# A two-layer diffusion backbone with expert lookup: one-hot products and low parts move from GpSimd to VectorE, one h tile in the second layer, own tokens finished in the last blocks

## The chip, the core and the metric

One core of a Trainium2 chip runs the whole program in one launch. The metric is the device time of that launch in microseconds (us). Engines are named as in the profile: PE is TensorE (PEld its weight loads), DVE is VectorE, ACT is ScalarE, POOL is GpSimd, SP is the engine that issues most DMAs. Every engine takes its instructions in order.

## The reference, cut to what matters

512 latent tokens and 256 context tokens, 1024 wide, pass two layers. Each layer has a mixer (attention and a gated delta net, not touched by the change) and then this lookup among 16384 experts; the second layer runs the lookup on the latent tokens alone.

```
q = (h @ wq).reshape(N, 8, 2, 128)
s = einsum('nhpd,hpkd->nhpk', q, keys)
top_s, top_i = top_k(s, 16)
cand_s = top_s[:, :, 0, :, None] + top_s[:, :, 1, None, :]
cand_i = top_i[:, :, 0, :, None] * 128 + top_i[:, :, 1, None, :]
best_s, best_pos = top_k(cand_s, 16)
idx, gate = take(cand_i, best_pos), softmax(best_s)
u, v = u_tab[idx], v_tab[idx]
act = gelu(einsum('tnd,td->tn', u, h))
f = einsum('tn,tnd->td', gate * act, v)
x = x + mod[5] * f
```

After the second layer the output is an RMSNorm of the latent x.

## The kernel before, in words

After the mixer, `merge` writes h (normed and modulated) transposed, as two float32r tiles, a high part and the rest: `h2hi/h2lo` for the first `nd` tiles of 128 tokens and `hghi/hglo` for the last `NG[l]` tiles (2 of 6 in the first layer, 1 of 4 in the second). Every product with h is three matmuls: high by high, low by high, high by low.

The tiles are treated in two ways. For the `nd` "dense" tiles the product of h with all 16384 expert rows is formed in 128 blocks of 128 experts (`peer_h`), and weighted by a dense gate matrix G that is mostly zero. For the last `NG[l]` "own" tiles the 128 chosen rows of each token are fetched by indirect DMA (`fetch`, issued by GpSimd), first rows of u with a row product on VectorE (`own_u`, tile `gb` or `gc`, L181), then rows of v with small matmuls (`own_v`).

The lookup of a layer (`peer`) has these stages:

- `scores`: 16 products of h with wq, each followed by products with the keys on PE and a top 16 on DVE.
- routing: for each tile `select` (DVE, with 14 small operations `rt__`, `rst` on GpSimd) picks 16 of the candidates per head; for a dense tile `spread` then builds its G: per 8 tokens four one-hot operations of 128x1024 halves (tile `oh`: two comparisons, two products), 16 small matmuls, and copies out by ACT. Every second of these groups has one product on GpSimd. `tick(2)` after each group moves the row fetches on by two.
- in the same stretch the first 80 blocks are multiplied ahead (`peer_h` with `lo_on="g"`): load 512 KB (`uraw`), `uhi` on ACT, `ulo` on GpSimd, 24 matmuls into bank `ip` or `sc`, gelu, store to DRAM (`He`).
- the main loop: 64 pairs of blocks, 24 pairs with their `peer_h`, 40 read back; each gives weights `Wh/Wl` and rows `vh/vl` and is multiplied out into PSUM (tiles 0 and 1 stay in banks `at`, `sc`; the others are added to `acc` on DVE). `due` spreads the remaining fetches over the loop.
- the end: the last two pairs are multiplied tile by tile, the result is gated and added to x and normed, in the order own tiles first, then moved and stayed tiles.

A scheduler fixes the order of the instructions on each engine when the program is built, from the order of the code and the life of the buffers; the `order` excerpts below show its results. Buffers `uhi`, `ulo` are two deep, `uraw` eight, `gb` three.

Of the kernel before, what the change touches and what calls it, by code (L numbers as in the profile page):

```python
# [108 lines left out]
class Ker:  # L109
# [234 lines left out]
    def norm_tile(self, pool, x, A, shift, hi, lo, toff, hi_on="v", lo_on="v", rows=None):  # L344

        ss = self.sm(1)
        sq = self.t(pool, [128, D], "nsq", bufs=1)
# [5 lines left out]
        y = self.t(pool, [128, D], "nxn", bufs=1)  # L353
        self.ts(y, x, r, None, ALU.mult)
# [656 lines left out]
    def merge(self, l, full, T, left, later, Gad, AT, BT, xin, xm, h2, S, N):  # L1011
# [4 lines left out]
        with ExitStack() as el:  # L1016
# [83 lines left out]
            hT = []  # L1100
            for st, nm, n in ((h2, "h2", nd), (hg, "hg", NG[l])):
                hp = st.enter_context(P(nm, S))
                hT.append([self.t(hp, [128, NCH, n * 128], f"{nm}{k}", F32R) for k in ("hi", "lo")])
            with P("mgo", S) as po:
# [22 lines left out]
                for i in range(nt):  # L1127
# [9 lines left out]
                    if i >= nd:  # L1137
                        rows[i] = self.t(self.dp, [128, D], f"hrow{l}_{i}")
                    seg, j = (hT[0], i) if i < nd else (hT[1], i - nd)
                    self.norm_tile(po, x, self.As[l][g][1], self.mods[l][g][:, 24:32], *seg, j * 128, rows=rows.get(i))  # L1140
# [3 lines left out]
    def scores(self, l, hT, T, tops, topi, N):  # L1144
# [4 lines left out]
        with ExitStack() as es:  # L1149
            qp = es.enter_context(self.tc.tile_pool(name=self.nm("rq"), bufs=1, side=N))  # L1150
            wp = es.enter_context(self.tc.tile_pool(name=self.nm("wq"), bufs=1, side=N))
            segs = ((hT[0], 0, T[0]), (hT[1], 512, T[1]))

# [94 lines left out]
    def spread(self, pool, ixs, gate, i, Gd, tick):  # L1248
# [19 lines left out]
        for half in range(2):  # L1268
            stg = self.t(pool, [128, 128, 64], "stg", bufs=2)
            for t8 in range(8):  # L1270
# [102 lines left out]
    def peer(self, l, hT, h2, hg, rows, groups, ahead, near, S, N):  # L1373
# [12 lines left out]
        with ExitStack() as es:  # L1386
# [4 lines left out]
            with P("rt", N) as pool:  # L1391
# [8 lines left out]
                with P("rt2", N) as rp:  # L1400
# [42 lines left out]
            W, Vv = [], []  # L1443
            units = ng * 256
            began = state[0]
            for n, b0 in enumerate(order):
# [10 lines left out]
                if n == len(order) - 2:  # L1457
# [5 lines left out]
                    for g, _, off in groups:  # L1463
                        for o in (0, 512):
                            gx = gates[g, o] = self.adw()
                            self.load(gx, self.gate_src(l, g, 5)[:, o:o + 512])
                            for i in moved:
                                if where[i][0] == g:
                                    a = acc[:, i - moved[0], o:o + 512]
                                    self.tt(a, a, gx, ALU.mult, eng=self.G)  # L1470
                if n < len(order) - 1:
                    W, Vv = [], []
# [42 lines left out]
            for i in range(nd):  # L1515
# [3 lines left out]
                else:  # L1519
                    x = self.t(self.wp, [128, D], "uraw", bufs=2)  # L1520
                self.load(x, xd[k * 128:(k + 1) * 128, :])
# [8 lines left out]
            fp = es.enter_context(tc.tile_pool(name=self.nm("pf"), bufs=1, side=S))  # L1530
            if last:
                fg = self.t(fp, [128, D], "fgrow")
                self.load(fg, self.I["fg"].broadcast_to([128, D]))
            todo = list(range(nd, nt)) + [i for j in range(max(len(moved), len(stay))) for i in (moved[j:j + 1] + [j] * (j < len(stay)))]
            banks = iter(("tp", "ip") * 2)
            ready = {}
            for n in range(nt + 1):
                if n < nt:
                    i = todo[n]
                    g, xd, k = where[i]  # L1540
                    x = ready[i] = self.t(fp, [128, D], "fx", bufs=3)
                    if i >= nd:
                        self.load(x, outs[i])
                        xs[i] = self.t(fp, [128, D], "fxr", bufs=2)
                        self.load(xs[i], xd[k * 128:(k + 1) * 128, :])
                        po = [(x[:, o:o + 512], o) for o in (0, 512)]
                    elif i in stay:
                        po = [(sums[i][:, o:o + 512], o) for o in (0, 512)]
                    else:
                        bank = next(banks)  # L1550
                        po = [(self.psum(bank), o) for o in (0, 512)]
                    for p, o in po:
                        if i < nd:
                            self.blocks(p, W, Vv, i, o, first=i not in stay)
                        self.tt(x[:, o:o + 512], p, gates[g, o], ALU.mult)
                        self.tt(x[:, o:o + 512], x[:, o:o + 512], xs[i][:, o:o + 512], ALU.add)
                if n == 0:
                    continue
                i = todo[n - 1]
                x = ready.pop(i)  # L1560
                g, _, k = where[i]
                if last:
                    sq = self.t(fp, [128, D], "nsq", bufs=2)
                    ss = self.sm(1)
                    self.act(sq, x, AF.Square, accum=ss)
                    self.ts(ss, ss, 1.0 / D, EPS, ALU.mult, ALU.add)
                    r = self.sm(1)
                    self.rsqrt(r, ss, 1)
                    self.stt(sq, x, r, fg, ALU.mult, ALU.mult)
                    self.load(self.out[k * 128:(k + 1) * 128, :], sq)  # L1570
                else:
                    self.load(xo[g][k * 128:(k + 1) * 128, :], x)
                    self.norm_tile(fp, x, self.As[l + 1][g][0], self.mods[l + 1][g][:, 0:8], nxt[0], nxt[1],
                                   i * 128, "s", "g" if n < nt else "v")
            main.close()
# [34 lines left out]
```

## Time and profile before

| | us |
|---|---|
| median of 3 runs (6343.70 to 6354.41) | 6346.27 |
| the profiled execution | 6341.51 |
| its span | 6339.7 |

| engine | busy us | share of the span |
|---|---|---|
| PE | 5720.0 | 90% |
| DVE | 4283.3 | 68% |
| POOL | 2542.7 | 40% |
| ACT | 2408.9 | 38% |

The profiled execution is 4.8 us under the median. A share of the whole span is a mean over stages: scores and routing of the first layer run from about 1415 to 2335 us of the span, its main loop to 3555 and its end to 3606; in the second layer scores begin at 4737, routing at 4886, the main loop at 5516, the end at 6302.

### The profile page before, as it was taken

Reading aid. Unit: us, or ns where it says so; the run is one execution under the profiler, and the core shown is the slowest. Engines: PE = TensorE matmul, PEld = TensorE weight load, DVE = VectorE, ACT = ScalarE, POOL = GpSimd, SP = SyncE. Lnnn points to the kernel's source line nnn. Section 1 sums busy time; section 2 is a strip of 40 time slices with the busy share of each in tenths; the row PEclk is TensorE's granted clock in tenths of the full one; section 3 lists DMA queues with packets and bytes.
Section 4 is the critical chain, followed back from the end, with each engine's and each line's share of the span. In section 5 each row is a group of like instructions: output and inputs, shape, how many; then the busy total and the mean of one; then the engine's idle time right before and its main releaser. Section 6 shows DMA issues by size and latency. Waiting matters only on the chain. (4 is left out here: it accounts for less than half of the span.)

```text
span 6339.7 us, 99239 instructions
## 1 busy us (share of the span) xinstructions
PE 5720.0 (90%) x36471; PEld 4739.1 (75%) x36471; DVE 4283.3 (68%) x8878; ACT 2408.9 (38%) x4336; POOL 2542.7 (40%) x2049
## 2 busy tenths in 40 slices
PE   8899999998877789999999798999998766899998
PEld 6888888786666667666666588888877766787776
DVE  5989875245889946665644589888555897555455
ACT  4554444232234522222332355444532343233333
POOL 2334333222687653333433333434432876602221
PEclk9999999999988899999999899999999888999999
DMA  5442323631466689999888444322431667867885
GB/s 193 137 144 95 99 87 115 212 115 56 155 222 245 228 301 319 326 331 315 307 295 287 161 163 137 109 95 95 137 132 62 203 223 299 291 204 270 275 274 195
DMA packets 567720, 1253.59 MB, mean 198 GB/s; under 512 B 65920, under 2 KB 228416, under 8 KB 565440
## 3 DMA queue, kind: packets, MB, share of 16 engines
q1 hardware_dynamic: 456640, 844.54, 39.6%
q0 software_dynamic: 110592, 402.70, 18.0%
q8 instruction: 287, 4.70, 0.3%
q14 instruction: 201, 1.65, 0.1%
HBM read 1049.76 MB, written 197.23 MB: 197 GB/s over the span
## 5 line engine op out<-in xcount | busy, mean ns | idle before, releaser
L167 POOL TENSOR_TENSOR wlo<-wraw,whi 128x512 fp32r<-128x512 f32 x418 | 570.7, 1369 | 1348.3 <-ACT whi L189 1205.2
L160 PE MATMUL ip<-hhi,whi 128*128 128x256 f32 x3120 | 734.3, 292 | 27.8 <-ACT ev L185 24.6
L160 PE MATMUL ip<-hlo,whi 128*128 128x256 f32 x3120 | 734.4, 291 | 0.0
L160 PE MATMUL ip<-hhi,wlo 128*128 128x256 f32 x3120 | 727.8, 291 | 5.7 <-POOL wlo L167 5.6
L160 PE MATMUL ip<-h2hi,ulo 128*128 128x512 f32 (+1 forms) x1408 | 537.1, 381 | 48.7 <-POOL ulo L167 47.9
L160 PE MATMUL ip<-h2hi,uhi 128*128 128x512 f32 (+1 forms) x1408 | 534.8, 380 | 44.6 <-ACT uhi L189 43.8
L181 DVE SCALAR_TENSOR_TENSOR gb<-gb,ghr 128x1024 f32<-128x1024 f32 x293 | 437.2, 1502 | 191.7 <-DMA gb<-in_ur_dram,gix 189.7
L160 PEld LDWEIGHTS ip<-hhi,whi 128*128 128x128 f32 x3120 | 519.4, 192 | 42.4 <-ACT ev L185 28.8
L160 PEld LDWEIGHTS ip<-hhi,wlo 128*128 128x128 f32 x3120 | 519.7, 192 | 16.6 <-POOL wlo L167 7.1
L160 PE MATMUL ip<-h2lo,uhi 128*128 128x512 f32 (+1 forms) x1408 | 528.2, 375 | 0.0
L160 PEld LDWEIGHTS ip<-hlo,whi 128*128 128x128 f32 x3120 | 522.1, 192 | 8.1 <-issue 0.2
L1294 POOL DMA_INDIRECT gc<-in_v_dram,gixT x221 | 243.6, 1102 | 656.0 <-PE tp L160 505.4
L1294 POOL DMA_INDIRECT gb<-in_ur_dram,gix x293 | 360.7, 1231 | 329.3 <-DVE gb L181 218.7
L167 DVE TENSOR_TENSOR acc<-acc,tp 128x512 f32<-128x512 f32 x366 | 247.8, 684 | 348.2 <-PE tp L160 311.9
L189 ACT CAST uhi<-uraw 128x1024 fp32r<-128x1024 f32 x256 | 268.7, 1051 | 549.2 <-PE ip L160 299.8
L167 POOL TENSOR_TENSOR ulo<-uraw,uhi 128x1024 fp32r<-128x1024 f32 x160 | 395.2, 2471 | 115.4 <-ACT uhi L189 112.7
L189 ACT CAST whi<-wraw 128x512 fp32r<-128x512 f32 x418 | 258.3, 621 | 474.7 <-PE at L160 188.1
L189 ACT CAST Wh<-ge 128x512 fp32r<-128x512 f32 (+1 forms) x256 | 144.5, 566 | 629.7 <-PE tp L160 294.9
L167 DVE TENSOR_TENSOR vl<-vraw,vh 128x1024 fp32r<-128x1024 f32 x256 | 311.7, 1232 | 76.1 <-ACT vh L189 75.4
L160 PEld LDWEIGHTS ip<-h2hi,ulo 128*128 128x128 f32 x1408 | 275.5, 196 | 113.2 <-POOL ulo L167 62.0
L160 PEld LDWEIGHTS ip<-h2hi,uhi 128*128 128x128 f32 x1408 | 276.8, 197 | 98.6 <-ACT uhi L189 49.5
L1294 POOL DMA_INDIRECT gb<-in_v_dram,gixT x163 | 179.1, 1099 | 418.0 <-PE tp L160 332.3
(455 smaller groups left out, 15469.4 us busy)
## 6 DMA issues: line engine op xcount, KB each, us to landing
uraw<-in_u_dram SPq DMA_DIRECT2D x256, 512.0 KB
vraw<-in_v_dram SPq DMA_DIRECT2D x256, 512.0 KB
wraw<-in_w_in_dram SPq DMA_DIRECT2D x288, 256.0 KB
G<-stg SPq DMA_DIRECT2D x14, 4096.0 KB
g<-G SPq DMA_DIRECT2D x896, 64.0 KB
adw<-in_w_ada_dram SPq DMA_DIRECT2D x192, 256.0 KB
raw<-ev SPq DMA_DIRECT2D x80, 384.0 KB
He<-ge SPq DMA_DIRECT2D x80, 256.0 KB
```

The lines of the kernel that those rows point to most:

```text
L160: self.PE.matmul(out, lhsT, rhs, start=start, stop=stop, skip_group_check=True, **k)
L167: (eng or self.V).tensor_tensor(out, a, b, op)
L181: eng.scalar_tensor_tensor(out, a, s, b, op0, op1, accum_out=accum)
L189: self.S.copy(hi, src)
L1294: self.G.indirect_dma_start(b, None, src, bass.IndirectOffsetOnAxis(ap=ix, axis=0))
```

## The change

- `merge`, `scores`: where all tiles fit 512 columns (the second layer), h is one pair of tiles and each wq product one 512-wide matmul instead of one of 384 and one of 128 columns.
- `spread`: all one-hot products on DVE; one or two fetches per group in turn instead of two.
- routing: `ulo` of the 80 blocks ahead on DVE instead of GpSimd.
- the end: own tiles are loaded, gated, added to x and normed (`norm_scale`) before the last two pairs; only their transposes (`norm_turn`) stay behind. In the end the dense tiles come first.

```diff
     def norm_tile(...):
+        r = self.norm_scale(x, self.t(pool, [128, D], "nsq", bufs=1))
+        y = self.t(pool, [128, D], "nxn", bufs=1)
+        self.ts(y, x, r, None, ALU.mult)
+        self.norm_turn(pool, y, A, shift, hi, lo, toff, hi_on, lo_on, rows)
...
# merge
-            for st, nm, n in ((h2, "h2", nd), (hg, "hg", NG[l])):
+            whole = nt * 128 <= 512
+            for st, nm, n in ((h2, "h2", nt),) if whole else ((h2, "h2", nd), (hg, "hg", NG[l])):
...
# scores
-            segs = ((hT[0], 0, T[0]), (hT[1], 512, T[1]))
+            segs = ((hT[0], 0, T[0]), (hT[1], 512, T[1])) if len(hT) > 1 else ((hT[0], 0, TT),)
...
# spread
-                self.tt(o4[:, 2], o4[:, 1], every(3, t), ALU.mult, eng=self.G if t8 % 2 else V)
+                self.tt(o4[:, 2], o4[:, 1], every(3, t), ALU.mult)
...
-                tick()
+                tick(1 + t8 % 2)
...
# peer
-                        self.spread(rp, *self.select(rp, tops[:, i], topi[:, i]), i, Gd, lambda: tick(2))
+                        self.spread(rp, *self.select(rp, tops[:, i], topi[:, i]), i, Gd, tick)
                 for b in range(ahead):
-                    ge = self.peer_h(l, b, hT, TT, lo_on="g")
+                    ge = self.peer_h(l, b, hT, TT)
...
# peer, ahead of the last two pairs
+                    for i in range(nd, nt):
+                        g, xd, k = where[i]
+                        x = own_y[i] = self.t(ap, [128, D], "gc", bufs=4)
+                        self.load(x, outs[i])
+                        x2 = self.t(self.gp, [128, D], "gb", bufs=3)
+                        self.load(x2, xd[k * 128:(k + 1) * 128, :])
+                        for o in (0, 512):
+                            self.tt(x[:, o:o + 512], x[:, o:o + 512], gates[g, o], ALU.mult)
+                        self.tt(x, x, x2, ALU.add)
+                        r = self.norm_scale(x, self.t(self.gp, [128, D], "gb", bufs=3))
...
+                            self.load(xo[g][k * 128:(k + 1) * 128, :], x)
+                            self.ts(x, x, r, None, ALU.mult)
...
# peer, the end
-            todo = list(range(nd, nt)) + [i for j in ...]
+            own = list(range(nd, nt))
+            todo = [i for j in range(max(len(moved), len(stay))) for i in (moved[j:j + 1] + [j] * (j < len(stay)))]
+            for n, i in enumerate(todo):
+                product(i)
+                if n:
+                    if own:
+                        turn(own.pop(0))
+                    finish(todo[n - 1])
```

GpSimd, first layer, while G is built (`ulo`, `oh` as above; `rst`, `rt__` are select's). Before:

```order
L1294 DMA gb_19865<-in_ur_dram,gix_18940 128x1024
L174 TENSOR_SCALAR rt__3779_19754<-rp_19751 128x128
L167 TENSOR_TENSOR ulo_22421<-uraw_22422,uhi_22420 128x1024
L167 TENSOR_TENSOR rst_19753<-rst_19753,rt__3779_19754 128x128
L1294 DMA gb_19893<-in_ur_dram,gix_18940 128x1024
L167 TENSOR_TENSOR oh_19230<-oh_19230,rdup_19186 128x1024
L174 TENSOR_SCALAR rt__3779_19754<-rp_19751 128x128
L1294 DMA gb_19896<-in_ur_dram,gix_18940 128x1024
L167 TENSOR_TENSOR ulo_22456<-uraw_22457,uhi_22455 128x1024
```

The changed program, same place:

```order
L1302 DMA gb_20508<-in_ur_dram,gix_18940 128x1024
L1302 DMA gb_20534<-in_ur_dram,gix_18940 128x1024
L174 TENSOR_SCALAR rt__3865_20315<-rp_20312 128x128
L1302 DMA gb_20537<-in_ur_dram,gix_18940 128x1024
L167 TENSOR_TENSOR rst_20314<-rst_20314,rt__3865_20315 128x128
```

The fetches no longer share their queue with `ulo` and `oh`; select's small operations stay.

DVE, first layer, while G is built. Before:

```order
L167 TENSOR_TENSOR oh_20050<-iota_68,rdup_19798 128x1024 x2
L179 SCALAR_TENSOR_TENSOR rk_3981_20970<-rp_20969,rk_3981_20970 128x128
L181 SCALAR_TENSOR_TENSOR gb_20442,ghc_19223<-gb_20442,ghr_19221 128x1024
L167 TENSOR_TENSOR oh_20050<-oh_20050,rdup_19798 128x1024
L179 SCALAR_TENSOR_TENSOR rk_3981_20970<-rp_20969,rk_3981_20970 128x128
L167 TENSOR_TENSOR oh_20019<-oh_20019,rdup_19798 128x1024
```

The changed program:

```order
L181 SCALAR_TENSOR_TENSOR gb_21122,ghc_19223<-gb_21122,ghr_19221 128x1024
L167 TENSOR_TENSOR ulo_23095<-uraw_23096,uhi_23094 128x1024
L167 TENSOR_TENSOR oh_19983<-oh_19983,rdup_19774 128x1024
L1218 MATCH_REPLACE rc_3952_20878<-rbs_20840,rcand_20830 128x50
L1218 MATCH_REPLACE rc_3953_20884<-rbs_20840,rcand_20830 128x50
L167 TENSOR_TENSOR oh_20014<-iota_68,rdup_19774 128x1024 x2
L167 TENSOR_TENSOR oh_19955<-oh_19955,rdup_19774 128x1024
```

`ulo` now stands among the one-hot operations and behind row products `gb`. In the first layer 76 `ulo` stand ahead of the last `oh` (25 of them ahead of the first), with 110 row products; in the second 30 stand among the top 16 of `scores`, 56 between there and the last `oh` (six of the 86 belong to the main loop), with 88 row products.

PE, second layer, in `scores` (`whi`, `wlo` are wq, `at` its bank). Before:

```order
L160 MATMUL at_49104<-hglo_47422,whi_49098 128x128
L160 MATMUL at_49104<-hghi_47421,wlo_49099 128x128
L160 MATMUL at_49156<-keys_49090,rq_49153 128x128 x4
L160 MATMUL at_49201<-h2hi_47416,whi_49189 128x384
L160 MATMUL at_49201<-h2lo_47417,whi_49189 128x384
```

The changed program:

```order
L160 MATMUL at_48579<-h2lo_47413,whi_48573 128x512
L160 MATMUL at_48579<-h2hi_47412,wlo_48574 128x512
L160 MATMUL ip_51457<-h2hi_47412,ulo_51452 128x384
L160 MATMUL ip_51457<-h2hi_47412,uhi_51451 128x384
L160 MATMUL ip_51457<-h2lo_47413,uhi_51451 128x384
```

Blocks multiplied ahead (`ip<-h2hi,ulo`) now stand between the 16 steps of `scores`; before, all 80 stood behind them. Behind the last one-hot matmul of the stage stood 16 blocks in the first layer and 32 in the second; now 5 and none.

## Rows read from the trace of the kernel before

**Rows 1.** Windows: stretch, us; busy PE, PEld, DVE, ACT, POOL; PEclk; DMA; GB/s

```profile
1620.00:2335.00 715.00, 574.10 (x2960) 455.76 (x2960) 591.35 (x1123) 272.14 (x293) 511.19 (x334) 0.89 0.69 239
1797.00:2195.00 398.00, 311.06 (x1846) 250.72 (x1844) 378.86 (x536) 177.30 (x180) 283.27 (x174) 0.87 0.65 229
2335.00:3555.00 1220.00, 1193.21 (x5396) 806.38 (x5397) 687.38 (x971) 341.35 (x485) 435.46 (x387) 0.99 0.87 304
4737.00:4886.00 149.00, 121.09 (x820) 116.20 (x817) 71.52 (x480) 34.68 (x75) 35.12 (x28) 0.99 0.18 58
4886.00:5516.00 630.00, 457.83 (x2715) 429.99 (x2716) 505.26 (x850) 228.62 (x261) 476.99 (x294) 0.86 0.71 248
5316.00:5516.00 200.00, 146.06 (x721) 137.08 (x721) 115.46 (x131) 49.30 (x65) 160.44 (x97) 0.90 0.93 329
5516.00:6302.00 786.00, 785.38 (x3921) 633.14 (x3920) 419.02 (x559) 289.80 (x413) 138.69 (x129) 1.00 0.75 250
```

**Rows 2.** DVE groups, 1620 to 2335: count | busy us, mean ns | idle before

```profile
L181 DVE SCALAR_TENSOR_TENSOR gb<-gb,ghr 128x1024 f32<-128x1024 f32 x125 | 188.2, 1516 | 80.8 <-DMA gb<-in_ur_dram,gix 80.4 <-DVE gb L181 0.4
L167 DVE TENSOR_TENSOR oh<-iota,rdup 128x1024 f16<-128x1024 f16 x128 | 135.6, 1106 | 10.9 <-ACT rdup L1258 5.8 <-PE at L160 2.7 <-PE tp L160 2.4
L167 DVE TENSOR_TENSOR oh<-oh,rdup 128x1024 f16<-128x1024 f16 x96 | 102.6, 1088 | 4.1 <-POOL oh L167 3.9
...
L179 DVE SCALAR_TENSOR_TENSOR rk<-rp,rk 128x128 f32<-128x128 f32 x42 | 27.2, 648 | 0.1
```

**Rows 3.** DVE groups, second layer, 4886 to 5516

```profile
L181 DVE SCALAR_TENSOR_TENSOR gb<-gb,ghr 128x1024 f32<-128x1024 f32 x106 | 173.4, 1649 | 91.2 <-DMA gb<-in_ur_dram,gix 91.0
L167 DVE TENSOR_TENSOR oh<-iota,rdup 128x1024 f16<-128x1024 f16 x96 | 101.2, 1101 | 4.0 <-PE at L160 2.4 <-PE tp L160 1.4
L167 DVE TENSOR_TENSOR oh<-oh,rdup 128x1024 f16<-128x1024 f16 x72 | 77.2, 1097 | 3.7 <-POOL oh L167 3.6
L181 DVE SCALAR_TENSOR_TENSOR gc<-gc,ghr 128x1024 f32<-128x1024 f32 x18 | 34.3, 1935 | 12.3 <-DMA gc<-in_ur_dram,gix 9.9 <-ACT ge L185 2.4
```

**Rows 4.** Instructions by tile, whole span: count, ns min/median/max, first and last start

```profile
L167 DVE TENSOR_TENSOR oh<-iota,rdup x224: 666/681/5119, 1797.3 to 5303.2; 128x1024 f16<-128x1024 f16 x112
...
L181 DVE SCALAR_TENSOR_TENSOR gb<-gb,ghr x293: 1197/1219/5697, 1677.7 to 5526.5; 128x1024 f32<-128x1024 f32 x147
...
L179 DVE SCALAR_TENSOR_TENSOR rk<-rp,rk x70: 265/290/3416, 1641.4 to 5134.6; 128x128 f32<-128x128 f32 x70
...
L167 DVE TENSOR_TENSOR ulo<-uraw,uhi x96: 1214/1226/1293, 2334.1 to 6252.1; 128x1024 fp32r<-128x1024 f32 x96
...
L160 PE MATMUL at<-keys,rq x320: 275/275/377, 1440.8 to 4886.8; 128*128 128x128 f32 x160
```

**Rows 5.** Timeline of DVE and POOL, 2000 to 2030: start, us, instruction

```profile
2001.19 3.74 DVE L167 TENSOR_TENSOR oh<-iota,rdup 128x1024 f16<-128x1024 f16 x2
2004.85 1.21 DVE L167 TENSOR_TENSOR re<-re,rti 128x2048 f16<-128x2048 f16 x1
...
2001.06 2.45 POOL L167 TENSOR_TENSOR ulo<-uraw,uhi 128x1024 fp32r<-128x1024 f32 x1
...
2004.53 1.23 POOL L1294 DMA_INDIRECT gb<-in_ur_dram,gix  x1
```

**Rows 6.** DVE groups in the main loop of the first layer, 2335 to 3555

```profile
L181 DVE SCALAR_TENSOR_TENSOR gc<-gc,ghr 128x1024 f32<-128x1024 f32 x73 | 88.9, 1220 | 32.3 <-DMA gc<-in_ur_dram,gix 32.3
```

**Rows 7.** PE timeline, 512-wide matmuls in an unbroken run of the main loop

```profile
3519.64 0.39 PE L160 MATMUL at<-vl,Wh 128*128 128x512 f32 x1
...
3525.08 0.39 PE L160 MATMUL tp<-vh,Wl 128*128 128x512 f32 x1
```

**Rows 8.** Chain that ended last, second layer: start, us, a 384-wide block

```profile
5616.21 4.19 PE ip L160 x24
```

**Rows 9.** DVE timeline at the two layers' ends

```profile
3563.12 1.29 DVE L167 TENSOR_TENSOR fx<-fx,adw 128x512 f32<-128x512 f32 x2 [5.47 <-DMA fx<-own]
...
6311.60 1.29 DVE L167 TENSOR_TENSOR fx<-fx,adw 128x512 f32<-128x512 f32 x2 [5.70 <-DMA fx<-own]
```

More of the change, by code (lines that the diff above doesn't have):

```diff
@@ L344, in norm_tile, with norm_scale @@
     def norm_tile(self, pool, x, A, shift, hi, lo, toff, hi_on="v", lo_on="v", rows=None):
+        r = self.norm_scale(x, self.t(pool, [128, D], "nsq", bufs=1))
+        y = self.t(pool, [128, D], "nxn", bufs=1)
+        self.ts(y, x, r, None, ALU.mult)
+        self.norm_turn(pool, y, A, shift, hi, lo, toff, hi_on, lo_on, rows)
+    def norm_scale(self, x, sq):
         ss = self.sm(1)
-        sq = self.t(pool, [128, D], "nsq", bufs=1)
         self.act(sq, x, AF.Square, accum=ss)
@@ L352, in norm_tile, with norm_turn @@
         self.rsqrt(r, v, 1)
-        y = self.t(pool, [128, D], "nxn", bufs=1)
-        self.ts(y, x, r, None, ALU.mult)
+        return r
+    def norm_turn(self, pool, y, A, shift, hi, lo, toff, hi_on="v", lo_on="v", rows=None):
         for c0 in (0, 4):
@@ L1138, in merge @@
                         rows[i] = self.t(self.dp, [128, D], f"hrow{l}_{i}")
-                    seg, j = (hT[0], i) if i < nd else (hT[1], i - nd)
+                    seg, j = (hT[0], i) if whole or i < nd else (hT[1], i - nd)
                     self.norm_tile(po, x, self.As[l][g][1], self.mods[l][g][:, 24:32], *seg, j * 128, rows=rows.get(i))
@@ L1444, in peer @@
             units = ng * 256
+            own_y, fg = {}, {}
             began = state[0]
@@ L1470, in peer @@
                                     self.tt(a, a, gx, ALU.mult, eng=self.G)
+                    if last:
+                        for o in (0, 512):
+                            fg[o] = self.adw()
+                            self.load(fg[o], self.I["fg"][:, o:o + 512].broadcast_to([128, 512]))
+                    for i in range(nd, nt):
[4 more added lines that the diff above has]
+                        self.load(x2, xd[k * 128:(k + 1) * 128, :])
+                        for o in (0, 512):
+                            self.tt(x[:, o:o + 512], x[:, o:o + 512], gates[g, o], ALU.mult)
+                        self.tt(x, x, x2, ALU.add)
+                        r = self.norm_scale(x, self.t(self.gp, [128, D], "gb", bufs=3))
+                        if last:
+                            for o in (0, 512):
+                                self.stt(x[:, o:o + 512], x[:, o:o + 512], r, fg[o], ALU.mult, ALU.mult)
+                            self.load(self.out[k * 128:(k + 1) * 128, :], x)
+                        else:
+                            self.load(xo[g][k * 128:(k + 1) * 128, :], x)
+                            self.ts(x, x, r, None, ALU.mult)
                 if n < len(order) - 1:
@@ L1519, in peer @@
                 else:
-                    x = self.t(self.wp, [128, D], "uraw", bufs=2)
+                    x = self.t(ap, [128, D], "gc", bufs=4)
                 self.load(x, xd[k * 128:(k + 1) * 128, :])
@@ L1530, in peer @@
             fp = es.enter_context(tc.tile_pool(name=self.nm("pf"), bufs=1, side=S))
[L1531 to L1560, printed above, removed]
@@ new lines, in peer, with product, turn @@
+            po = {}
+            def product(i):
+                if i in stay:
+                    po[i] = [(sums[i][:, o:o + 512], o) for o in (0, 512)]
+                else:
+                    po[i] = [(self.psum("ip"), o) for o in (0, 512)]
+                for p, o in po[i]:
+                    self.blocks(p, W, Vv, i, o, first=i not in stay)
+            def turn(i):
+                if not last:
+                    g = where[i][0]
+                    self.norm_turn(fp, own_y[i], self.As[l + 1][g][0], self.mods[l + 1][g][:, 0:8], nxt[0], nxt[1],
+                                   i * 128, "s", "g")
@@ L1561, in peer, with finish @@
+            def finish(i, lo_on="g"):
                 g, _, k = where[i]
+                x = self.t(fp, [128, D], "fx", bufs=3)
+                for p, o in po.pop(i):
+                    self.tt(x[:, o:o + 512], p, gates[g, o], ALU.mult)
+                    self.tt(x[:, o:o + 512], x[:, o:o + 512], xs[i][:, o:o + 512], ALU.add)
                 if last:
                     sq = self.t(fp, [128, D], "nsq", bufs=2)
-                    ss = self.sm(1)
-                    self.act(sq, x, AF.Square, accum=ss)
@@ L1566, in peer @@
[L1566 to L1569, printed above, removed]
+                    r = self.norm_scale(x, sq)
+                    for o in (0, 512):
+                        self.stt(sq[:, o:o + 512], x[:, o:o + 512], r, fg[o], ALU.mult, ALU.mult)
                     self.load(self.out[k * 128:(k + 1) * 128, :], sq)
@@ L1573, in peer @@
                     self.norm_tile(fp, x, self.As[l + 1][g][0], self.mods[l + 1][g][:, 0:8], nxt[0], nxt[1],
-                                   i * 128, "s", "g" if n < nt else "v")
+                                   i * 128, "s", lo_on)
+            own = list(range(nd, nt))
[6 more added lines that the diff above has]
+                    finish(todo[n - 1])
+            for i in own:
+                turn(i)
+            finish(todo[-1], "v")
             main.close()
```

## The prediction, before the changed kernel was run

> **What bounds the kernel now.** I read the windows by stage first, then the DVE groups of the routing stretches, then single instructions. In the main loops PE is the bound: 1193 of 1220 us in the first layer, 785 of 786 in the second [rows 1]; only less PE work shortens them. Routing is another matter. In the first layer it takes 715 us, with PE busy for 574 of them at a granted clock of 0.89 and DVE for 591; in the middle of it, while G is built, DVE is busy for 379 of 398 us [rows 1]. In the second layer routing takes 630 us, with DVE at 505 and PE at 458, and in its last 200 us, when G is complete, neither is the bound: DVE 115, PE 146, GpSimd 160, DMA at 0.93 [rows 1]. So DVE bounds the larger part of routing, and GpSimd with its queue of `ulo` and fetches the rest.
>
> The reader should see next that much of DVE's time there is no work. A comparison `oh` takes 681 ns in the median of all [rows 4], but 1106 in the mean of the first layer's routing and 1101 in the second's [rows 2, 3]; the row product `gb` takes 1219 in the median [rows 4], 1516 and 1649 in the mean [rows 2, 3]. Where the rest comes from shows in the timeline: two `oh` that began beside a 2.45 us `ulo` on GpSimd took 3.74 us together where 1.3 is usual, and a `re` that ran beside a fetch took 1.21 [rows 5]. In the main loop, where GpSimd does little but fetch, 73 row products have a mean of 1220 ns [rows 6], so fetches don't stretch them. My reading: DVE waits for GpSimd's elementwise operations, and not for its fetches.
>
> **First layer, scores to main loop.** Stretch over the medians [rows 2, 4]: `gb` 125 x 0.297 = 37 us, `oh` comparisons 128 x 0.425 = 54, `oh` products 96 x 0.407 = 39 (by the comparison's median, the same shape), `rk` 42 x 0.358 = 15; together 146. `rt__` and `rst` of select stay on GpSimd, so I let a tenth stay and take out 131. Added to DVE: 80 `ulo` at 1.226 us [rows 4] = 98, and 32 `oh` at 0.681 = 22. Moved out: the order has 110 row products ahead of the last `oh`, where 125 ran in this stretch [rows 2]; 15 x 1.22 = 18 us. DVE then needs 591 - 131 + 98 + 22 - 18 = 562 us, less than before although 120 us of work came to it. What share of the stretch it can fill is unknown. The nearest rows are 0.83 (591 of 715, with the waits for fetched rows) and 0.95 (379 of 398) [rows 1]; `ulo` brings DVE new waits for ACT and PE, but GpSimd's queue is free for fetches, so I take 0.90, between the two. 562/0.90 = 624 us, a gain of 91 on 715; 38 and 123 at the ends. PE's need is no more than its 574 busy us, which includes time at the lower clock, and stays under 624.
>
> **Second layer, scores to main loop.** The 779 us from 4737 are 149 of scores and 630 of routing [rows 1]. In scores, 384 pairs of a 384- and a 128-wide matmul become 384 of 512 columns. A 512-wide one issues every 0.227 us (24 steps in 5.44 us) [rows 7], so 87 us, with 64 matmuls with keys at 0.275 [rows 4] 18 more: 105, where 121 are busy now [rows 1]. Between them now stand 30 blocks of 4.19 us [rows 8] = 126 us, which also fill the 28 idle us. Scores become 231 us. Routing: stretch [rows 3, 4] `gb` 106 x 0.430 = 46, `oh` 96 x 0.420 = 40 and 72 x 0.416 = 30, `gc` 18 x 0.716 = 13, in all 129; a tenth stays, 116 go. Added: 56 `ulo` = 69 us and 24 `oh` = 16. Row products fall from 124 to 88: 36 x 1.22 = 44 out. DVE needs 505 - 116 + 69 + 16 - 44 = 430, at 0.90 478 us. In sum 709 against 779, a gain of 70. With 0.80 (505 of 630) it is 10, with 0.95 it is 95. Six `ulo` of that stretch belong to main-loop blocks; that loop is PE alone, so 6 x 4.19 = 25 us more come off it.
>
> **The ends.** Own tiles leave the tail: waits of DVE for their loads of 5.5 and 5.7 us [rows 9], and per tile two such pairs of 1.29 us [rows 9], 5.2 in the first layer (two tiles), 2.6 in the second; 19 us. Their work goes into the last pairs at no cost, covered by PE, while DVE is busy for about half of the main loop (687 of 1220) [rows 1]. The added waits: the products with the own rows stand on DVE ahead of the last `vl` and `Wl`, and their loads on SP ahead of the last pairs' loads. If such a load is late, PE waits for `vl` behind it, and the 11 us are only moved. Between 0 and 19 I take 15, as the loads are asked for a pair earlier.
>
> **The main loops.** The 15 fetches put off in the first layer are 0.5 MB each (128 rows of 4 KB), 7.9 MB; at 304 GB/s [rows 1] 26 us if nothing hides them, 0 if all is hidden. DMA is at 0.87 there and PE idle for 27 us; I take 8. In the second layer 36 fetches go into a loop with DMA at 0.75 under a full PE [rows 1]: nothing, and 75 us at its 250 GB/s if that cover were gone. The other edits (buffers' pools, the final gain read by halves) cost nothing, as they add no instruction of size where something waits.
>
> **Sum.** -91 - 70 - 25 - 15 + 8 = -193 us against the profiled execution's 6341.5, so 6148.5. The median of the runs is 4.8 above that execution; the forecast for the median is **6153 us**. With all terms at their poor ends it is 6299, at their good ends 6084.
>
> **Rivals.**
> - *The stretch stays* (slower). If fetches, or the select operations that remain, hold DVE up as `ulo` did, DVE keeps 131 and 116 us and gets the new work on top. First layer 693/0.90 = 770, 55 more than now; second 546/0.90 + 231 = 838, 59 more; with -25, -15 and +8 it is 82 slower, 6428 us. It decides where over 70% of the 247 us stay, since each is worth 1/0.90 us and 193 us are to be lost. For it: DVE is full at 379 of 398 and gets 120 us more [rows 1]. Against it: 1220 ns beside fetches [rows 6]. Chance 0.08. The Trainium skill ("Perfetto Trace Analysis", "Optimizing Scalar/DVE Operations") says that when DVE is saturated, handing some of its work to ScalarE or even GpSimd may make sense, and adds that GpSimd and DVE share a read port, so that handing work between those two might not help. By the first half alone this change goes the wrong way and 6428 is its time; the rows on the stretch bear out the second half.
> - *DVE's queue is the new wait.* `ulo` stands behind row products, and DVE idled 81 and 91 us for fetched rows in these stretches [rows 2, 3]; before, `ulo` on GpSimd did not stand behind them. PE would wait for `ulo`, and utilization stay at 0.83 and 0.80: 53 and 60 us worse, 6266. Against it: the fetch no longer stands behind a 2.45 us `ulo` [rows 5]. Chance 0.20.
> - *Given back later.* The routing gains come, but the fetches put off show fully in the first layer's loop (26 in place of 8) and the own loads hold the last pairs: 6153 + 18 + 15 = 6186. Chance 0.10.
> - *Better.* DVE fills 0.95 throughout, as it did while building G: 32 and 25 us more, 6096. Chance 0.14.
>
> **How the numbers follow.** The forecast has 0.48. Its own spread from the utilization alone reaches from about 6110 to 6215. The range of 8 in 10, 6075 to 6275, takes in the better case and the queue's case and leaves out the slower one and the far tails. A measurement of this kernel can tell about 0.2%, 13 us, from no change. Faster by more than that: forecast, better case, giving back, and most of the queue's case, 0.88; within it 0.04; slower 0.08, the rival with the stretch.
>
> **What would show it.** Right: in the routing of both layers the mean `oh` near 0.7 us and `gb` near 1.22; DVE's `ulo` near 1.23; routing near 624 us in the first layer; scores of the second near 231 with PE almost without a gap, and scores and routing together near 709; no wait for `fx<-own` at the ends. Wrong: `oh` still above 1 us in the mean (stretch stays); PE's longest wait in routing for DVE `ulo` with DVE idle for `gb` (queue); PE idle in the first main loop well above 27 us (given back).

## The result, and the profile after

| | us |
|---|---|
| before, median of 4 runs beside the change | 6349.44 |
| changed kernel, median of 4 runs (6078.54 to 6089.81) | 6084.19 |
| ratio, 95% interval | 0.9583, 0.9566 to 0.9599 |
| profiled execution of the change | 6081.79 |
| its span | 6080.0 |

The kernel is 265 us faster; the forecast was 193 us faster, its range reached down to 6075. The sign and the mechanism held, the size did not: the gain is 1.4 times the forecast.

To see where it came from I cut both traces at the same matmuls: the last product with keys and the first product of the main loop in the first layer, the first product of the next mixer, the first wq product of the second layer, the first of its main loop.

| stretch | before | after | difference | forecast |
|---|---|---|---|---|
| to the first layer's last keys | 1619.5 | 1618.0 | -1.5 | 0 |
| routing, first layer | 729.6 | 602.8 | -127 | -91 |
| main loop and end, first layer | 1257.7 | 1258.1 | 0 | -8 + 8 |
| mixer, to the first wq product | 1114.1 | 1126.0 | +12 | 0 |
| scores and routing, second layer | 802.3 | 657.1 | -145 | -70 |
| main loop and end, second layer | 816.5 | 818.0 | +1.5 | -25 - 7 |

The forecast's stretches were cut at round times, 715 and 779 us, so 15 and 23 us of what this table calls routing lay outside them. The second row of the table and the fifth are these windows of the kernel before (columns as in [rows 1]):

```profile
1619.00:2349.00 730.00, 587.77 (x3022) 466.68 (x3022) 599.31 (x1134) 277.07 (x300) 515.88 (x337) 0.89 0.69 240
4721.00:4887.00 166.00, 137.52 (x912) 131.82 (x912) 80.07 (x500) 41.22 (x92) 39.69 (x31) 0.97 0.19 60
4887.00:5523.00 636.00, 463.83 (x2749) 436.07 (x2749) 510.98 (x858) 230.61 (x264) 480.31 (x297) 0.87 0.71 249
```

and these of the changed kernel, with G being built (1805 to 2186) and the main loops besides:

```profile
1618.00:2221.00 603.00, 542.16 (x3007) 435.84 (x3008) 519.90 (x1212) 272.83 (x294) 234.73 (x211) 0.95 0.77 269
1805.00:2186.00 381.00, 347.32 (x2211) 280.87 (x2211) 340.02 (x605) 204.69 (x210) 119.79 (x104) 0.96 0.80 284
2221.00:3463.00 1242.00, 1211.31 (x5415) 811.44 (x5415) 725.09 (x1046) 353.64 (x505) 454.47 (x402) 1.00 0.88 311
4605.00:4825.00 220.00, 218.24 (x1167) 199.81 (x1165) 104.67 (x511) 77.47 (x120) 36.10 (x28) 1.00 0.41 134
4825.00:5262.00 437.00, 317.56 (x2149) 299.89 (x2148) 389.42 (x879) 188.28 (x212) 181.29 (x164) 0.86 0.79 276
5230.00:5262.00 32.00, 0.18 (x3) 0.04 (x1) 12.80 (x24) 3.90 (x5) 14.64 (x13) 0.50 0.93 351
5262.00:6063.00 801.00, 783.92 (x3873) 627.12 (x3873) 455.74 (x640) 289.81 (x413) 167.28 (x156) 0.99 0.79 268
```

In the first layer DVE runs 1212 instructions where it ran 1134, and is busy for 520 us in place of 599: more work in less time. GpSimd falls from 516 to 235 us. PE's busy share rises from 0.81 to 0.90 and its granted clock from 0.89 to 0.95 (nearer to the level of 2.4 GHz), and about the same number of matmuls takes 542 us in place of 588. While G is built, PE is now busy for 347 of 381 us and DVE for 340; before it was 311 and 379 of 398 [rows 1]. What the change lost shows in the sixth row: 32 us in which PE does nothing and DMA is at 0.93.

The DVE groups of the first layer's routing, 1618 to 2221, answer to [rows 2]:

```profile
L181 DVE SCALAR_TENSOR_TENSOR gb<-gb,ghr 128x1024 f32<-128x1024 f32 x110 | 134.6, 1228 | 32.8 <-DMA gb<-in_ur_dram,gix 32.7
L167 DVE TENSOR_TENSOR ulo<-uraw,uhi 128x1024 fp32r<-128x1024 f32 x82 | 100.2, 1222 | 33.3 <-ACT uhi L189 33.2
L167 DVE TENSOR_TENSOR oh<-oh,rdup 128x1024 f16<-128x1024 f16 x128 | 83.9, 686 | 0.3
L167 DVE TENSOR_TENSOR oh<-iota,rdup 128x1024 f16<-128x1024 f16 x128 | 83.1, 702 | 9.0 <-PE tp L160 3.5 <-ACT rdup L1266 3.0 <-PE at L160 2.5
```

Every mean is at the median of the kernel before [rows 4]: `oh` 686 and 702 ns in place of 1088 and 1106, `gb` 1228 in place of 1516. DVE's wait for fetched rows fell from 81 to 33 us, as the fetches no longer stand behind `ulo` on GpSimd (57 us again with `ulo` put back, below); a wait of 33 us for `uhi` is new. In the second layer, 4825 to 5262, against [rows 3]:

```profile
L181 DVE SCALAR_TENSOR_TENSOR gb<-gb,ghr 128x1024 f32<-128x1024 f32 x95 | 116.7, 1230 | 37.1 <-DMA gb<-in_ur_dram,gix 36.9
L167 DVE TENSOR_TENSOR ulo<-uraw,uhi 128x1024 fp32r<-128x1024 f32 x58 | 71.0, 1225 | 8.3 <-ACT uhi L189 8.3
L167 DVE TENSOR_TENSOR oh<-oh,rdup 128x1024 f16<-128x1024 f16 x96 | 63.2, 687 | 0.0
L167 DVE TENSOR_TENSOR oh<-iota,rdup 128x1024 f16<-128x1024 f16 x96 | 62.3, 698 | 3.5 <-PE at L160 2.0 <-PE tp L160 1.5
```

What PE waited for in the first layer's routing of the kernel before, 1619 to 2349 (total us, times, longest):

```profile
PE at L160 <- DVE oh L167: 42.6, 15, 7.9
PE tp L160 <- DVE oh L167: 26.0, 10, 5.4
PE sc L160 <- POOL ulo L167: 22.7, 14, 3.4
PE ip L160 <- POOL ulo L167: 13.9, 14, 2.4
```

In the changed kernel the 69 us for `oh` are gone from this stretch. The 37 us for GpSimd's `ulo` are not: 39 us for DVE's `ulo` took their place. PE's idle time in the stretch fell by 81 us in all, most of it these waits for the one-hot products.

Two new waits of PE stand on the other side. The first lies ahead of the second layer's scores (waits of PE, 4560 to 4640: total, times, longest):

```profile
PE tp L164 <- DVE nxn L172: 11.7, 2, 10.7
```

With one h tile the first wq matmul needs all four token tiles, so it stands behind the norm of the last one. The second lies at the start of the main loop. The chain that ended last, around 5215 to 5275, and PE's timeline there (start, us, instruction, idle before it):

```profile
5232.15 15.48 DMA G<-stg
...
5251.68 7.65 DMA g<-G
...
5263.46 14.40 DMA g<-G
```

```profile
5261.99 1.19 PE L160 MATMUL tp<-vh,Wh 128*128 128x512 f32 x2 [31.82 <-ACT vh L189]
5284.79 1.22 PE L160 MATMUL tp<-vh,Wh 128*128 128x512 f32 x2 [13.04 <-ACT vh L189]
```

G goes out to DRAM and comes back before the first pair can be weighted; the row names ACT's `vh`, but the chain shows the two transfers as what came last. Before, 32 blocks stood behind the last one-hot matmul and PE worked on them meanwhile. Now none does, and PE idles for 31.8 and 13.0 us.

### The profile page after: what moved, and what is told of

Its sections match the earlier page's. It is cut to its first block, busy times and chain, and to the rows that moved or that the text cites. A ratio compares the mean times of both kernels' runs of the same rounds, so it can differ in the third digit from the quotient of the medians.

```text
span 6080.0 us, 98316 instructions
## 1 busy us (share of the span) xinstructions
PE 5620.5 (92%) x36087; PEld 4639.6 (76%) x36087; DVE 4169.0 (69%) x9095; ACT 2407.6 (40%) x4320; POOL 2008.7 (33%) x1833
## 5 line engine op out<-in xcount | busy, mean ns | idle before, releaser
L167 POOL TENSOR_TENSOR wlo<-wraw,whi 128x512 fp32r<-128x512 f32 x418 | 571.9, 1371 | 1390.3 <-ACT whi L189 1257.7
L160 PE MATMUL ip<-h2hi,ulo 128*128 128x512 f32 (+1 forms) x1408 | 521.4, 371 | 32.9 <-DVE ulo L167 32.9
L160 PE MATMUL ip<-h2hi,uhi 128*128 128x512 f32 (+1 forms) x1408 | 522.3, 371 | 29.6 <-ACT uhi L189 28.9
L1302 POOL DMA_INDIRECT gb<-in_ur_dram,gix x261 | 330.2, 1265 | 517.2 <-DVE gb L181 346.9
L167 DVE TENSOR_TENSOR ulo<-uraw,uhi 128x1024 fp32r<-128x1024 f32 x256 | 312.8, 1222 | 248.4 <-ACT uhi L189 243.0
L1302 POOL DMA_INDIRECT gc<-in_v_dram,gixT x218 | 229.6, 1053 | 450.0 <-PE tp L160 291.2
L181 DVE SCALAR_TENSOR_TENSOR gb<-gb,ghr 128x1024 f32<-128x1024 f32 x261 | 319.5, 1227 | 79.3 <-DMA gb<-in_ur_dram,gix 79.0
L167 DVE TENSOR_TENSOR vl<-vraw,vh 128x1024 fp32r<-128x1024 f32 x256 | 311.1, 1228 | 61.6 <-ACT vh L189 61.6
L160 PE MATMUL tp<-vh,Wh 128*128 128x512 f32 x744 | 293.7, 399 | 61.2 <-ACT vh L189 46.6
L189 ACT CAST vh<-vraw 128x1024 fp32r<-128x1024 f32 x256 | 263.7, 1046 | 169.4 <-PE sc L160 70.6
```

The source lines that it names most:

```text
L160: self.PE.matmul(out, lhsT, rhs, start=start, stop=stop, skip_group_check=True, **k)
L167: (eng or self.V).tensor_tensor(out, a, b, op)
L181: eng.scalar_tensor_tensor(out, a, s, b, op0, op1, accum_out=accum)
L189: self.S.copy(hi, src)
L1302: self.G.indirect_dma_start(b, None, src, bass.IndirectOffsetOnAxis(ap=ix, axis=0))
```

## The experiments

My theory: GpSimd's elementwise operations held DVE up (the stretch), and stood in the same queue as the fetches; taking `ulo` and `oh` off it removes both. The rivals to it: the gain is mostly the one h tile or the ends; or it is only the queue and not the stretch; or the stretch comes from any GpSimd work. Differences below are against 6084 us; the kernel before moved by 3 us between the groups of runs (6346.4 to 6349.8), so a few us say nothing.

| edit of the changed kernel | us | ratio to before, 95% interval | against 6084 |
|---|---|---|---|
| `ulo` ahead back on GpSimd | 6227.96 | 0.9804, 0.9781 to 0.9828 | +144 |
| every second `oh` product back on GpSimd | 6144.97 | 0.9683, 0.9665 to 0.9701 | +61 |
| both | 6278.45 | 0.9886, 0.9869 to 0.9903 | +194 |
| two h tiles again | 6130.72 | 0.9657, 0.9641 to 0.9674 | +47 |
| own tiles behind the last pairs again | 6095.37 | 0.9594, 0.9579 to 0.9609 | +11 |
| extra GpSimd operations without an input | 6165.07 | 0.9712, 0.9695 to 0.9729 | +81 |
| the same, reading `uhi` | 6214.08 | 0.9786, 0.9771 to 0.9801 | +130 |
| select's operations on DVE | 6083.04 | 0.9579, 0.9565 to 0.9594 | -1 |
| 96 blocks ahead in the second layer | 6074.53 | 0.9569, 0.9555 to 0.9582 | -10 |
| first wq products split | 6087.72 | 0.9577, 0.9561 to 0.9592 | +4 |
| split and 96 blocks | 6075.34 | 0.9563, 0.9550 to 0.9576 | -9 |

**`ulo` back on GpSimd.**

```diff
-                    ge = self.peer_h(l, b, hT, TT)
+                    ge = self.peer_h(l, b, hT, TT, lo_on="g")
```

> The changed kernel, with ulo of the 80 blocks ahead back on GpSimd in both layers. Stretch theory (DVE is held while GpSimd reads tiles): 160 GpSimd operations of about 2.4 us return, the mean oh in the routing of both layers rises from 0.69-0.70 us to 0.95 or more, the mean gb from 1.23 to over 1.4, and the program takes 90 to 160 us more than the changed kernel's 6084, 6174 to 6244. Queue theory (only ulo's place behind fetches in GpSimd's queue cost time): the same rise in time, but PE's waits for ulo are over 100 us in sum and DVE is under 0.8 busy while G is built. One-tile theory (the gain is from blocks multiplied during scores): under 30 us, 6084 to 6114.

It costs 144 us, 98 of them in the first layer's routing (701 us), 24 in the second's scores and routing, the rest mostly in the main loop behind. The window and the DVE groups, 1622 to 2323:

```profile
1622.00:2323.00 701.00, 575.00 (x3022) 455.11 (x3021) 585.25 (x1162) 277.33 (x299) 439.69 (x302) 0.92 0.73 246
```

```profile
L181 DVE SCALAR_TENSOR_TENSOR gb<-gb,ghr 128x1024 f32<-128x1024 f32 x110 | 159.6, 1457 | 57.4 <-DMA gb<-in_ur_dram,gix 57.1 <-DVE gb L181 0.2
L167 DVE TENSOR_TENSOR oh<-iota,rdup 128x1024 f16<-128x1024 f16 x128 | 126.3, 1035 | 5.8 <-PE at L160 3.4 <-PE tp L160 2.3
```

and what PE waits for there:

```profile
PE sc L160 <- POOL ulo L167: 36.7, 21, 4.5
PE ip L160 <- POOL ulo L167: 31.8, 16, 8.5
```

DVE has 80 operations of 1.2 us less in each layer and still the time rises: the `oh` comparisons are at 1035 ns again (the products at 899), `gb` at 1457, and a `ulo` takes GpSimd 2497 ns where DVE needs 1222. In this stretch DVE is busy for 585 us against 520, 65 more although some 95 us of `ulo` left it, and idle for 33 us more, of which 24 are waits for fetched rows. In the second layer the means of `oh` (926 and 939 ns) stay a little under the 0.95 us that the stretch theory asked for. PE's wait for `ulo` in the first layer is 68 us against 39 in the changed kernel:

```profile
PE sc L160 <- DVE ulo L167: 22.6, 12, 7.1
PE ip L160 <- DVE ulo L167: 16.2, 8, 5.9
```

So the rival in which DVE's queue becomes the new wait is half there (39 us of waits for a `ulo` of DVE exist); with `oh` on DVE and only `ulo` on GpSimd, GpSimd's queue is the longer one. The queue theory asked for waits for `ulo` of over 100 us and for DVE under 0.8 busy while G is built: the waits come to 99 us over both layers, just short of it, but DVE is 0.90 busy (378 of 420 us).

**Every second `oh` product back on GpSimd.**

```diff
-                self.tt(o4[:, 2], o4[:, 1], every(3, t), ALU.mult)
+                self.tt(o4[:, 2], o4[:, 1], every(3, t), ALU.mult, eng=self.G if t8 % 2 else V)
```

> The changed kernel, with every second one-hot product back on GpSimd (56 of 2.2 us). Stretch theory: DVE saves 56 x 0.68 = 38 us and is held up by roughly half of 56 x 2.2 us = 60 us; the mean of the other oh rises to 0.8 or more and the program takes 10 to 50 us more, 6094 to 6134. Queue theory: nobody waits long for these products, within 15 us of 6084, on the faster side.

61 us, more than either theory expected (10 to 50 us more, and within 15), for 56 operations that on DVE cost 38 us: in the first layer a GpSimd `oh` takes 2360 ns, and DVE's own rise to 804 and 935 ns, as the stretch theory had it.

**Both back.**

> ulo of the blocks ahead and every other comparison oh are both put back on GpSimd; all else stays as changed. Theory (one shared cause, GpSimd's reads that hold DVE up and its queue): the costs of the two, 144 and 61 us, hardly overlap or add to each other; together 190 to 220 us over the changed kernel, 6275 to 6305. Rival (what one of them stretches or blocks is already stretched or blocked by the other): below 175 over it.

194 us, against 205 for the sum of the two: they hardly overlap, as the theory had it. The window of the first layer's routing is back at the kernel before, GpSimd's 531 us included:

```profile
1616.00:2358.00 742.00, 588.83 (x3023) 468.35 (x3023) 616.04 (x1146) 277.03 (x300) 531.45 (x343) 0.89 0.69 241
```

By the marks that stretch takes 742 us in this kernel, 730 before, and PE waits for `oh` of DVE again, 77 us in it. So its whole gain comes from these two moves. With the h tile (47) and the ends (11), 252 of the 265 us are accounted for, if the parts add up. What else the change holds, one or two fetches per group in place of two and other buffers, was not undone by itself.

**Which GpSimd operations hold DVE up.** Two kernels put work on GpSimd that the lookup does not need: twice per block ahead, GpSimd fills or overwrites `ge` before the gelu writes it. One fills with zeros, the other reads `uhi`.

```diff
-                    ge = self.peer_h(l, b, hT, TT)
+                    ge = self.peer_h(l, b, hT, TT, fill=2)
...
+        for _ in range(fill):
+            self.G.memset(ge, 0.0)
```

> The changed kernel with 160 added GpSimd operations in each layer, two per block multiplied ahead, that only write: a memset of the block's output tile ge (128x512, 128x384 in the second layer) ahead of its gelu. Read-port reading of the stretch theory (a DVE operation with two inputs waits only for GpSimd operations that read): oh stays at 0.69-0.71 us in the mean, the program within 25 us of 6084, what is lost coming from ACT's gelu waiting for GpSimd. Any-operation reading (DVE waits for whatever GpSimd runs): oh rises to 0.78 or more, 40 to 120 us more.

```diff
+            self.G.tensor_scalar(ge, hi[:, :TT], 1.0, None, ALU.mult)
```

> The same 160 added GpSimd operations in each layer, but a product by 1 that reads uhi and writes ge. Nothing on PE or DVE gets its data from them. Stretch theory in both readings: oh in the mean 0.78 us or more in the routing of both layers, gb 1.3 or more, 40 to 120 us more than 6084. Queue theory (only what waits for GpSimd's results pays): as the run with writes, within 25 us of 6084, the two runs within 15 us of each other.

The filling kernel, first layer's routing: DVE's `oh`, then GpSimd's fills in the groups of that engine.

```profile
L167 DVE TENSOR_TENSOR oh<-oh,rdup 128x1024 f16<-128x1024 f16 x128 | 84.1, 686 | 0.2
L167 DVE TENSOR_TENSOR oh<-iota,rdup 128x1024 f16<-128x1024 f16 x128 | 83.7, 702 | 11.1 <-PE at L160 6.1 <-PE tp L160 5.0
```

```profile
L1371 POOL MEMSET ge<- 128x512 f32 x159 | 83.7, 529 | 156.2 <-DMA He<-ge 150.0 <-ACT uhi L189 2.5 <-ACT stg L185 0.3
```

No stretch at all beside 159 GpSimd operations: 686 and 702 ns, the same as without them. The timelines of the two kernels show it on single instructions. Filling:

```profile
2025.60 1.16 POOL L1371 MEMSET ge<- 128x512 f32 x2
...
2025.64 1.27 DVE L167 TENSOR_TENSOR oh<-iota,rdup 128x1024 f16<-128x1024 f16 x2
```

Reading `uhi`:

```profile
2010.86 1.52 POOL L1371 TENSOR_SCALAR ge<-uhi 128x512 f32<-128x512 f32 x1
2013.58 1.21 POOL L1302 DMA_INDIRECT gb<-in_ur_dram,gix  x1 [1.19 <-DVE gb L181]
...
2010.01 2.04 DVE L167 TENSOR_TENSOR oh<-iota,rdup 128x1024 f16<-128x1024 f16 x2
...
2013.23 1.28 DVE L167 TENSOR_TENSOR oh<-iota,rdup 128x1024 f16<-128x1024 f16 x2
```

Two `oh` take 1.27 us beside the fills and 1.28 beside a fetch, 2.04 beside an operation that reads. Over the first layer's routing the means in the reading kernel are 779 and 788 ns, `gb` 1316. The Trainium skill ("SBUF — State Buffer", "Who interferes with whom") states this rule: a DVE instruction with two inputs in SBUF contends with a GpSimd instruction that reads SBUF, not with one that only writes it. These runs agree, 686 ns against 779.

The filling kernel is 81 us slower all the same, where up to 25 were expected with `oh` unstretched. In the first layer 150 us of GpSimd's idle time end with the store of an earlier `ge` (`He<-ge`), while the fetches stand behind in its queue. DVE's wait for fetched rows grows from 33 to 53 us, and ACT's gelu waits for the fill. So an operation on GpSimd that stretches nothing can still cost, through what it makes wait. The 49 us between the two kernels are no price of the stretch either. The reading operation takes 1708 ns where a fill takes 529, and ACT waits longer for it; first the filling kernel, then two rows of the reading one, first layer's routing:

```profile
ACT ge L185 <- POOL ge L1371: 17.7, 4, 6.0
```

```profile
ACT ge L185 <- POOL ge L1371: 145.6, 25, 15.3
ACT uhi L189 <- POOL ge L1371: 46.7, 13, 8.5
```

In the second layer the reading kernel's `oh` are at 750 and 756 ns, short of the 780 that were expected in both, and its 130 us lie over the 40 to 120. So what the two kernels show is which operations stretch DVE's, not how many us that costs. They don't divide the 144 us of `ulo` between stretch and queue: a fill waits for `ge`, where `ulo` waited for `uhi` (88 us in the first layer of the run with `ulo` back). That division stays open.

**Select's small operations on DVE.**

```diff
-            self.ts(t, p, float(ROW_S[r]), float(ROW_N[r - 1]), ALU.is_ge, ALU.mult, eng=G)
-            self.tt(st, st, t, ALU.add, eng=G)
+            self.ts(t, p, float(ROW_S[r]), float(ROW_N[r - 1]), ALU.is_ge, ALU.mult)
+            self.tt(st, st, t, ALU.add)
```

> The changed kernel with select's 14 small operations per tile on DVE too, so that GpSimd has only fetches and one cast per tile in routing. Stretch theory: the last stretch goes (about 13 us of 520 in the first layer, less in the second), 84 and 56 operations of 0.16 to 0.28 us come to DVE (13 to 24 and 9 to 16 us), the chain of select gets shorter by its trips between engines: within 15 us of 6084. A fall of over 15 us would say that trips to GpSimd bound select; a rise of over 15 us that DVE alone bounds routing.

No difference. The tenth of the stretch that the prediction kept for these operations is not there.

**Two h tiles again.**

```diff
-            whole = nt * 128 <= 512
+            whole = False
```

> The changed kernel, with h of the second layer in two pairs of tiles as before. One-tile theory, as the forecast's sum has it: no block can be multiplied during scores, 24 blocks stand behind the last one-hot matmul again, scores and routing of the second layer take 60 to 110 us more than their 657 us, 6145 to 6195. Stretch theory alone (DVE bounds routing, the order of blocks is free): under 30 us more, as the blocks behind the last one-hot matmul fill the 32 us gap that opened there. First layer the same in both.

47 us slower. From the first wq product to the main loop it takes 735 us against 657, 78 more; the mixer ahead is 11 us shorter and the main loop 14. PE's wait for the last norm is gone (4545 to 4620):

```profile
PE tp L164 <- DVE nxn L172: 1.0, 1, 1.0
```

So the one h tile is worth 47 us net, and pays 11 for standing behind the norm. The rise in scores and routing is the expected one (60 to 110); what the mixer and the main loop gave back was not expected.

**The ends.** The block of own tiles that the diff of the change adds ahead of the last two pairs is put behind them, ahead of the dense tiles, with the norm still apart:

```diff
-                    for i in range(nd, nt):
...
+            for i in range(nd, nt):
```

> The changed kernel, with the own tiles loaded, gated, summed and normed behind the last pairs again, ahead of the dense tiles. The forecast had 15 us for it: 6099. If, as a look at the two traces suggests, the end gained little (the time from the main loop's start to the second layer's scores did not shrink), within 8 us of 6084.

11 us, where the prediction took 15 for it. The two kernels' intervals overlap (0.9579 to 0.9609 against 0.9566 to 0.9599), so the size is not clear of the noise.

**Filling the two new waits.** First 96 blocks ahead in the second layer in place of 80:

```diff
-            xin, hT = self.peer(l, hT, h2, hg, rows, groups, (80, 80)[l], near, S, N)
+            xin, hT = self.peer(l, hT, h2, hg, rows, groups, (80, 96)[l], near, S, N)
```

> The changed kernel with 96 instead of 80 blocks multiplied ahead in the second layer. In the changed kernel PE stands still for 32 us between the last one-hot matmul and the main loop, while G goes to DRAM and back, and is idle for a quarter of the routing behind scores. With 16 more blocks 10 stand behind the last one-hot matmul: 42 us of PE work over the gap, and the main loop of the second layer loses 16 x 4.19 = 67 us of PE work. Theory of the exposed round trip: 15 to 45 us less, 6039 to 6069. Rival (DVE bounds routing, each ulo put there costs 1.2 us and DMA in the main loop rises): within 12 us of 6084.

Only 10 us, within the 12 that the rival allowed. The trace is of the slowest of its five executions (6094 us). The 45 us wait is gone from it (the longest that is left in the main loop is 4.3 us) and 10 blocks stand behind the last one-hot matmul, but PE waits for their rows. The window behind that matmul, and what PE waits for from the first wq product to the main loop:

```profile
5253.00:5323.00 70.00, 47.12 (x220) 44.33 (x220) 35.50 (x48) 20.22 (x25) 23.92 (x21) 0.83 1.00 381
```

```profile
PE ip L160 <- ACT uhi L189: 26.3, 14, 5.1
PE sc L160 <- ACT uhi L189: 24.8, 6, 8.8
```

DMA is at 1.00 and 381 GB/s there, with G's round trip and the blocks' rows in the same window. PE waits for `uhi` for 51 us (18.5 in the changed kernel): one wait took the place of the other. Then the first two wq products of the second layer in two pieces, so that PE starts on 384 columns while the last tile is normed:

```diff
-            for h, o, n in segs:
+            head = segs if len(hT) > 1 else ((hT[0], 0, TT - 128), (hT[0], TT - 128, 128))
+            for h, o, n in head:
...
-                    self.proj([(ps[:, o:o + n], 0, n)], w, h)
+                    self.proj([(ps[:, o:o + n], o if len(hT) == 1 else 0, n)], w, h)
```

> In the second layer the first two heads' wq matmuls are split into columns 0 to 384 and 384 to 512, so that PE has work while the last tile is still being normed. Theory (the 10.7 us that PE waits for nxn ahead of the scores is a loss of the one wide tile): the wait falls to about 1 us and the time by about 10 us from 6084, to 6073. Rival (given back in the routing, which DVE sets, or no work is there before the norm): within 5 us of the changed kernel.

> The same split, and 96 blocks in place of 80 ahead of the second layer's main loop. Theory (two separate idle stretches of PE, 11 us ahead of the scores and 45 us around the first pair's G): the gains of the two add up, 10 + 10 = 20 us less than the changed kernel, about 6064. Rival (blocks taken into the routing only lengthen it, as the 96 alone suggest): no better than the split alone.

The split alone is worth nothing. Waits of PE in this kernel, 4560 to 4825:

```profile
PE at L160 <- ACT whi L189: 3.7, 1, 3.7
PE at L160 <- ACT rs L1188: 2.5, 2, 1.8
PE tp L164 <- DVE nxn L172: 1.1, 1, 1.1
```

The wait for `nxn` fell from 11.7 to 1.1 us and scores start 9 us sooner after the mixer, but they take 230 us in place of 220: 6 us are new waits for `whi` and `rs`, and PE is busy for 257 us of this stretch in place of 251, with 51 more matmuls. With both edits the time is that of the 96 blocks alone, 12 us under the split alone and 11 over the sum that the theory asked for. Neither of the two waits could be had back whole; the 96 blocks gain 10 us at most, and their interval overlaps the changed kernel's.

## Why the prediction was right, and where its sizes were off

- **The mechanism.** Right in the main. DVE waits for GpSimd's elementwise operations that read, and not for its fetches; with `ulo` and `oh` gone from GpSimd the means fall to the medians, and putting both back undoes the first layer's gain. Elementwise operations of GpSimd that only write stretched nothing (`oh` at 686 and 702 ns beside the fills).
- **DVE's need in the first layer, 562 us.** Measured 520. The tenth of the stretch that was kept (15 us) went too, and the list of stretched groups was short: `gb`, `oh` and `rk` were in it, but the others shrank as well, `re` from 39 to 30 us and the 54 `rcand` from a mean of 380 ns to 208.
- **The share that DVE fills, 0.90.** Measured 520 of 603, 0.86. So the better case (0.95 throughout) did not come; the time was better because the need was smaller. The 0.95 of [rows 1] was itself made of stretch: without it, DVE fills 340 of 381 us in the same place, 0.89, with PE at 0.91. 624 us were forecast and 603 measured; of the 36 us between -91 and -127, 21 are this, and 15 lay behind the forecast's cut at 2335, where it let them stand.
- **The second layer's scores, 231 us, and routing, 478.** Measured 220 and 437, 52 us less in all; 23 more are the cut. 27 blocks ran in the scores where 30 were counted, PE busy for 218 of 220 us. DVE's need was 389 us, not 430: again the tenth (13), and `rk` (23 to 9 us) and `re`, left out of that layer's list, while 98 row products (95 `gb`, 3 `gc`) ran where 88 were counted. That routing came out at 437 although PE is idle in its last 32 us and DVE busy for 13 of them.
- **Six blocks less in the second main loop, -25.** Wrong. By the trace 44 blocks ran in it and 46 before, two less, 8 us. And the step missed what the order showed: none of the blocks stood behind the last one-hot matmul any more. Their work was counted as filling the gaps ahead; that they also covered G's round trip was not. It costs 31.8 us ahead of the loop and 13.0 in it.
- **The ends, -15.** The experiment says 11, not clear of the noise. The waits for `fx<-own` of 5.5 and 5.7 us are gone; DVE waits 0.9 and 2.3 us for the same loads ahead of the last pairs.
- **The put-off fetches, +8.** The first layer's loop and end together stayed at 1258 us, where -8 and +8 were forecast; the rival in which gains are given back there did not come.
- **Not in the sum.** 12 us ahead of the scores, from the single h tile; the diff named the tile, and what becomes its first consumer was not asked.
- **The rivals.** The slower one, with the stretch staying, fell with the first `oh` row. The queue on DVE is there by the very sign that was written down for it: PE's longest waits in the first layer's routing are for DVE's `ulo` (39 us), with DVE idle for `gb` (33 us). It did not decide the time, as PE had waited 37 us for GpSimd's `ulo` before and lost the 69 us for `oh`.
- **Luck.** The sum of all terms at their good ends, 6084, is the measured time, but not by its terms: the two routings gained 127 and 145 us where 123 and 95 were their good ends, and the second main loop gave nothing of its 25. Errors of both signs cancelled.

## What to carry to other kernels

A busy engine is not an engine at work: compare the mean of an operation with its median, group by group and for all groups, before deciding that the engine is full; here taking work off the emptier engine and giving it to the one that looked full was worth 194 us. Before moving work out of a stretch's tail, ask which transfer it covered. A wait that is filled with work which needs the same resource (here DMA at 1.00) only changes its name.

## What the runs showed of the hardware that was not expected

- 159 GpSimd fills of 529 ns stretch no `oh` at all (686 and 702 ns), reading operations do (779 and 788 ns): the stretch comes from what GpSimd reads, not from its being busy.
- GpSimd fills that took 84 us in the first layer and 67 in the second, and stretched no `oh`, made the program 81 us slower: they waited for a buffer with the fetches behind them, and ACT waited for them.
- A `ulo` takes 2497 ns on GpSimd and 1222 on DVE.
- The same 3000 matmuls of the first layer's routing took 588 us of PE at a granted clock of 0.89 and 542 at 0.95: the prediction had left that busy time as it was. The clock rose as PE's idle time in the stretch fell from 142 to 61 us; no run shows what the higher clock by itself was worth to the stretch.
